# Sums over features by token in a Hyena and DeltaNet layer: which operand of the product is stationary

## Chip, core and metric

The kernel runs on one core of a Trainium2 chip (trn2). The metric is the device time of one execution in microseconds; three runs give 3350.19, 3352.44 and 3355.91 us, and their median, 3352.44 us, is the time before.

## What is computed

One trunk layer is applied to 128 context tokens and 256 latent tokens, 384 in all, of 2048 features each: a half-step SwiGLU, a token mixer (Hyena and gated DeltaNet side by side) and a second half-step SwiGLU. Each sub-layer stands between two RMS norms, and in the DeltaNet q and k are normalised per head:

```python
def rms_norm(x, g):
    y = xf * lax.rsqrt(jnp.mean(xf * xf, axis=-1, keepdims=True) + RMS_EPS)
    return (y * g.astype(jnp.float32)).astype(x.dtype)

def l2_norm(x):
    return x * lax.rsqrt(jnp.sum(x * x, axis=-1, keepdims=True) + RMS_EPS)

def trunk_layer(...):
    h = adaln(x, norm_pre[0], mod[:, :, 0], mod[:, :, 1])
    x = x + 0.5 * mod[:, :, 2] * rms_norm(swiglu(h, ...), norm_post[0])
    h = adaln(x, norm_pre[1], mod[:, :, 3], mod[:, :, 4])
    ...    # y: Hyena (with a norm of its own) and DeltaNet, times w_out
    x = x + mod[:, :, 5] * rms_norm(y, norm_post[1])
    h = adaln(x, norm_pre[2], mod[:, :, 6], mod[:, :, 7])
    x = x + 0.5 * mod[:, :, 8] * rms_norm(swiglu(h, ...), norm_post[2])
```

All inputs are float32. The change concerns the sums over features that these norms need.

## The kernel before

Activations lie with features on the partitions: a tile is 128 features by 384 tokens (T), and 16 tiles (KT) make the 2048 features. Weights come from DRAM in units of 512 rows by 256 columns (`unit`, line 122 and below), are split into two float32r parts, `hi` (ScalarE, line 122) and `lo` (VectorE or GpSimd, line 123), and each product of 128 x 128 weights with a tile is three TensorE instructions, lines 146 to 148, of 384 columns each.

The stages in order of time are: the start up to about 190 us (loading and transposing x, the first norm, the modulation's first quarter-blocks, lines 285 to 298, and the filter spectra of the Hyena between them), the first FFN, a bridge, the Hyena (to about 1630 us), the DeltaNet scans of four pairs of heads, the output projection `w_out`, a second bridge, the second FFN and the output.

A sum over features runs across partitions, so TensorE does it. Three places need one:

- `rms` (line 353) for the norm of x at the start (16 tiles) and the Hyena's output norm (8 tiles, line 1166). ScalarE squares a tile (line 361), and TensorE multiplies it by a stationary block of ones of 32 columns (line 363), each tile to one of four quarters of the partitions of one PSUM bank. Then the sums are copied to SBUF (line 365), three products with a column of constants bring them to one value per token (line 368), GpSimd raises these to the power -1/2 (line 371), and `spread` (line 445) copies them to all partitions.
- `fold` and `fold_end`: beside the last down-projection of the first FFN (fold 1), beside `w_out` (fold 2) and beside the last down-projection of the second FFN (fold 3). For each tile of the result y, folds 1 and 2 sum y^2, x y' and y'^2 (lines 418, 427, 429), one kind to each quarter of the partitions; tiles 0 to 11 are first added in pairs on GpSimd (line 437), and the last four tiles go singly. That makes 30 sums. Fold 3 has 16 sums of y^2 alone. The product is in `add_sum`, line 412. `fold_end` copies the sums out (line 454), transposes them to tokens (line 465; in fold 3 line 460) and computes the factors on VectorE and GpSimd (lines 461 to 473). `bridge` spreads them, updates x and makes the operands of the next sub-layer.
- `gdn_pair`: squared norms of q and k of two heads, four tiles (line 825), copied (827), transposed (829) and used from line 833 on.

In the down-projection the sums of one step of 256 columns are handed out behind the products of the next step, so those of the last four tiles stand behind the last product. The program is written in order and a scheduler of the framework, which has its own model of durations, sets the order on each engine. Every engine takes its instructions in that order. The modulation's weight blocks (512 KB) go through a ring of four buffers (`aw`, line 285) on SP's DMA queue.

Of the kernel before, what the change touches and what calls it, by code (L numbers as in the profile page):

```python
# [19 lines left out]
P = 128  # L20
# [24 lines left out]
def constants():  # L45
    """Tables that depend on the shapes alone."""
# [23 lines left out]
    # per level the couples within a block of 2s whose halves differ  # L70
# [10 lines left out]
    # Transforms at the odd frequencies pi (f + 1/2) / n, where the products of a signal's and a filter's lags below n  # L81
    # don't wrap. The latent ones take the even and the odd tokens apart: they give f and, with the other sign, n - 1 - f.
# [22 lines left out]
class Builder:  # L105
# [19 lines left out]
    def unit(self, src, cols=256):  # L125
        """Rows (k p) x columns of a weight, as two float32r parts whose sum is the weight."""
# [23 lines left out]
    def proj(self, mats, xh, xl, order=(0, 1, 2, 3)):  # L150
        """For each (weight, first column): two tiles [128 features, T] of weight^T x; with a third entry, the
        number of columns, one tile of so many features."""
        mats = [(m + (256,))[:3] for m in mats]
        res = [[self.acc() for _ in range(max(1, m[2] // P))] for m in mats]
        for a, kg in enumerate(order):
            us = [self.unit(w[kg * 512:kg * 512 + 512, c0:c0 + n], n) for w, c0, n in mats]
            for k in range(4):
                kk = kg * 4 + k
                for pts, u, m in zip(res, us, mats):
                    for n, pt in enumerate(pts):  # L160
                        wd = min(P, m[2])
# [5 lines left out]
    def setup(self):  # L167
# [5 lines left out]
        small = cst.tile([P, 4], F32, name="small")  # L173
        nc.vector.memset(small[:, 0:1], 2.0 ** -16)
        nc.vector.memset(small[:, 1:2], 2.0 ** -15)
        nc.vector.memset(small[:, 2:4], -0.5)
        self.c_d, self.c_dh = small[:, 0:1], small[:, 1:2]
# [18 lines left out]
        # groups of at most 128 rows for a transpose each, the first of the conditioning alone  # L196
# [27 lines left out]
        # silu of the conditioning, as the stationary operand of the modulation (columns: context, latent)  # L224
# [129 lines left out]
    def rms(self, pool, get, n, const, ring):  # L354
        """The mean square over features plus eps, per token, [128, 3], and its -1/2nd power for every partition, [128, T]
        in PSUM; get(i): the i-th of n tiles."""
        nc = self.nc
        ps = self.aux("sums")
        for i in range(n):
            sq = ring()  # L360
            nc.scalar.activation(out=sq, in_=get(i), func=AF.Square)
            q = 32 * (i % 4)
            nc.tensor.matmul(ps[q:q + 32, :T], self.ones[:, :32], sq, start=i < 4, stop=i >= n - 4)
        sb = ring()
        nc.vector.tensor_copy(out=sb, in_=ps[:, :T])
        pt = self.aux("tok")
        for t in range(3):
            nc.tensor.matmul(pt[:, t:t + 1], sb[:, t * P:t * P + P], const, start=True, stop=True)
        r = pool.tile([P, 2, 3], F32, tag="r6", name="r6", bufs=1)
        nc.vector.tensor_scalar(out=r[:, 0], in0=pt[:, :3], scalar1=EPS, scalar2=None, op0=ALU.add)  # L370
# [3 lines left out]
    def coef(self, pool, i):  # L374
        """Scale of the i-th pre-norm, [128, group, KT]."""
# [30 lines left out]
        # the modulation's accumulator is free  # L406
# [4 lines left out]
    def add_sum(self, q, first, last, sq):  # L411
        self.nc.tensor.matmul(self.f["ps"][32 * q:32 * q + 32, :T], self.ones[:, :32], sq, start=first, stop=last)  # L412

    def fold(self, k, y):
        """What tile k of y adds to the sums."""
# [3 lines left out]
        if f["last"]:  # L419
            for v, (a, b) in enumerate(SEG):  # L420
                nc.vector.tensor_scalar(out=y[:, a:b], in0=y[:, a:b], scalar1=f["pg"][:, v, k:k + 1], scalar2=None, op0=ALU.mult)
            return [(k % 4, k < 4, k >= KT - 4, sq)]
# [8 lines left out]
        if k < KT - 4:  # L431
            # TensorE takes the sums of two tiles
# [6 lines left out]
        return [(q, k < 2, k == KT - 1, a) for q, a in enumerate(new)]  # L439

    def spread(self, r):
        """[128 tokens, 3] -> the same for every partition, [128, T] in PSUM."""
# [5 lines left out]
    def fold_end(self):  # L448
        """Per token: factor of the post-norm and, but for the last, of the pre-norm after it."""
        nc, f = self.nc, self.f  # L450
        tt, ts, st = nc.vector.tensor_tensor, nc.vector.tensor_scalar, nc.vector.scalar_tensor_tensor
        n = P if f["last"] else 96
        sb = f["ring"]()
        nc.vector.tensor_copy(out=sb[:n], in_=f["ps"][:n, :T])
        pt = self.aux("tok")
        r = f["pool"].tile([P, 3, 3], F32, tag="r3", name="r3", bufs=1)
        r1, r2, s = r[:, 0], r[:, 1], r[:, 2]
        if f["last"]:
            for t in range(3):
                nc.tensor.matmul(pt[:, t:t + 1], sb[:, t * P:t * P + P], self.c_d, start=True, stop=True)  # L460
            ts(out=s, in0=pt[:, :3], scalar1=EPS, scalar2=None, op0=ALU.add)
            nc.gpsimd.tensor_tensor(out=r1, in0=s, in1=self.mhalf[:, :3], op=ALU.pow)
            return r1, None
# [4 lines left out]
        nc.gpsimd.tensor_tensor(out=r1, in0=s, in1=self.mhalf[:, :3], op=ALU.pow)  # L468
        tt(out=s, in0=m[:, :, 2], in1=r1, op=ALU.mult)
# [6 lines left out]
    def bridge(self, pool, x, y, i):  # L476
        """x += r1 y', and the operands of the next sub-layer, the i-th, a tile of features at a time."""
# [109 lines left out]
    def sine(self, out, x, bias):  # L587
        """out = sin(x + bias), the argument brought to [-pi, pi] first."""
# [16 lines left out]
    def filters(self, pool, loads):  # L605
        """Filter spectra of both sequence lengths, without their normalisation, into DRAM; its inverse stays. Yields between its
        parts."""
# [14 lines left out]
        def last_layer(o, half):  # L622
            """The last layer's columns of a filter and half of the channels, both directions, twice."""
# [16 lines left out]
        # the second layer's output twice, on either half of the partitions: [h; h] and its float32r parts [hi; hi], [lo; 0]  # L640
# [28 lines left out]
            # sum and difference of both directions: context, even and odd latent tokens  # L669
# [56 lines left out]
    def conv3(self, u, pt, w):  # L726
        """u = centred width-3 convolution along the tokens of pt, within each group; w(j): [128, 1]."""
# [8 lines left out]
    def gates(self, pl, pt):  # L736
        """Decay and beta of every (direction, chunk, head), per token, and what the chunks need of them."""
# [20 lines left out]
        # softplus(x) = max(x, 0) + 2 atanh(e / (2 + e)) with e = exp(-|x|)  # L758
# [33 lines left out]
    def gdn_pair(self, pl, p, hh, hl, out):  # L792
        """q, k and v of a pair of heads and what its scan needs of them, into out; yields after q and after k."""
# [5 lines left out]
        # one slot of 24 KB holds, for two pairs in turn, q and k by feature and k and v by token  # L799
# [7 lines left out]
        for i in range(3):  # L807
# [20 lines left out]
            for t in range(3):  # L828
                nc.tensor.transpose(pn[:, t * P:t * P + P], sq[:, t * P:t * P + P], self.ident)
# [499 lines left out]
```

## Time and profile before

| what | value |
|---|---|
| median of three runs | 3352.44 us |
| profiled execution, first to last instruction | 3349.9 us |
| TensorE busy (matmul) | 3268.2 us, 98% |
| VectorE busy | 2150.9 us, 64% |
| ScalarE busy | 1109.6 us, 33% |
| GpSimd busy | 228.5 us, 7% |
| TensorE's clock, mean of what was granted | 0.989 |

PE stands for TensorE's matmuls and PEld for its loading of the stationary operand, which overlaps them; DVE is VectorE, ACT is ScalarE, POOL is GpSimd and SP issues DMAs. Products are pipelined, so their durations overlap, and a busy share of 98% does not say how densely they are issued: for that the starts of neighbours are compared. A float32 product of this kernel appears as two instructions in the trace; a float32r product and a transpose appear as one.

### The profile page before, as it was taken

The numbers are of one execution on the slowest core, as the hardware profiler recorded it, in microseconds if no ns is written. First come the engines' busy times: TensorE is split into PE (matmuls) and PEld (weight loads), VectorE is DVE, ScalarE is ACT, GpSimd is POOL, SyncE is SP. The second block draws the span as 40 slices with busy tenths as digits, with TensorE's granted clock in tenths as the row PEclk, the third lists the DMA queues.
The fourth block names the chain that finished last, engine by engine and source line by source line (L and its number), as shares of the span: only waits on it lengthen the run. The fifth ranks groups of instructions, "written<-read, shape, count | busy, mean of one in ns | idle before, by whom it ended". The sixth has DMA issues, their size and how long they took to land.

```text
span 3349.9 us, 47713 instructions
## 1 busy us (share of the span) xinstructions
PE 3268.2 (98%) x19174; PEld 3098.8 (93%) x19174; DVE 2150.9 (64%) x3042; ACT 1109.6 (33%) x1602; POOL 228.5 (7%) x249
## 2 busy tenths in 40 slices
PE   5899999999999999999999999989999999999998
PEld 2499999999999997999999999979999999999997
DVE  4579978879786957777656665479544433444434
ACT  4432222222222225433333333353222222222223
POOL 1100000000000003100122321120000000000000
PEclk8999999999999999999999999999999999999999
DMA  9867767667665742543322234338444333444442
GB/s 308 289 200 251 251 193 227 220 203 247 225 220 175 253 143 82 180 124 113 120 76 70 76 95 145 112 109 268 149 129 128 126 126 126 126 127 126 129 129 83
DMA packets 423798, 542.71 MB, mean 162 GB/s; under 512 B 20292, under 2 KB 373882, under 8 KB 422936
## 3 DMA queue, kind: packets, MB, share of 16 engines
q1 hardware_dynamic: 413072, 522.27, 48.8%
q10 hardware_dynamic: 8232, 11.40, 1.0%
q0 software_dynamic: 2272, 5.98, 0.6%
q8 instruction: 151, 2.47, 0.3%
q14 instruction: 71, 0.58, 0.1%
HBM read 524.38 MB, written 15.20 MB: 161 GB/s over the span
## 4 chain that ended last, share of the span: by engine, by line
PE 92%; DVE 4%; DMA 2%; issue 1%; ACT 1%; POOL 0%; ACTq 0%; DVEq 0%; SPq 0%; POOLq 0%
PE mm L146 27%; PE mm L148 27%; PE mm L147 27%; DMA aw<-in_ada_w_dram 2%; PE sums L412 1%; PE pb L1058 1%; PE pb L1053 1%; PE ada L291 1%; DVE acc L327 1%; DVE lo L123 1%; PE aux L1100 1%; PE aux L1124 1%; PE pa L334 1%; DMA slot<-in_hy_decay_dram 1%; PE aux L716 0%
## 5 line engine op out<-in xcount | busy, mean ns | idle before, releaser
L123 DVE TENSOR_TENSOR lo<-raw,hi 128x1024 fp32r<-128x1024 f32 (+1 forms) x676 | 825.8, 1223 | 679.7 <-ACT hi L122 664.5
L146 PE MATMUL mm<-hh,hi 128*128 128x384 f32 x3728 | 1247.8, 338 | 7.6 <-ACT hh L122 6.3
L147 PE MATMUL mm<-hl,hi 128*128 128x384 f32 x3728 | 1253.1, 336 | 0.7 <-POOL hl L123 0.3
L122 ACT CAST hi<-raw 128x1024 fp32r<-128x1024 f32 (+1 forms) x676 | 707.3, 1047 | 1617.6 <-PE mm L147 1460.1
L148 PE MATMUL mm<-hh,lo 128*128 128x384 f32 x3728 | 1238.8, 337 | 2.4 <-DVE lo L123 2.4
L146 PEld LDWEIGHTS mm<-hh,hi 128*128 128x128 f32 x3728 | 700.2, 188 | 18.5 <-ACT hh L122 8.2
L148 PEld LDWEIGHTS mm<-hh,lo 128*128 128x128 f32 x3728 | 699.2, 188 | 13.1 <-issue 6.7
L147 PEld LDWEIGHTS mm<-hl,hi 128*128 128x128 f32 x3728 | 701.1, 188 | 8.8 <-issue 4.9
L327 DVE SCALAR_TENSOR_TENSOR acc<-aw,cs,acc 128x1024 f32<-128x1024 f32 x420 | 519.4, 1277 | 33.7 <-DMA aw<-in_ada_w_dram 33.0
L148 PE MATMUL mm<-gh,lo 128*128 128x384 f32 x1408 | 472.7, 336 | 1.5 <-DVE lo L123 1.5
L146 PE MATMUL mm<-gh,hi 128*128 128x384 f32 x1408 | 474.1, 337 | 0.0
L147 PE MATMUL mm<-gl,hi 128*128 128x384 f32 x1408 | 472.1, 335 | 0.0
L538 DVE TENSOR_TENSOR yacc<-mm,yacc 128x384 f32<-128x384 f32 x320 | 171.4, 554 | 166.5 <-PE mm L148 166.5
L146 PEld LDWEIGHTS mm<-gh,hi 128*128 128x128 f32 x1408 | 264.3, 188 | 13.7 <-issue 7.7
L148 PEld LDWEIGHTS mm<-gh,lo 128*128 128x128 f32 x1408 | 264.2, 188 | 7.8 <-issue 5.0
L147 PEld LDWEIGHTS mm<-gl,hi 128*128 128x128 f32 x1408 | 264.3, 188 | 2.5 <-issue 2.5
L437 POOL TENSOR_TENSOR sqs<-sqs 128x384 f32<-128x384 f32 x36 | 44.3, 1241 | 1174.3 <-DMA raw<-in_ffn_wd_dram 1080.1
L148 PE MATMUL mm<-yh,lo 128*128 128x384 f32 x256 | 85.8, 339 | 0.0
L147 PE MATMUL mm<-yl,hi 128*128 128x384 f32 x256 | 85.8, 336 | 0.0
L513 ACT ACTIVATE sg<-mm 128x384 f32<-128x384 f32 x88 | 43.3, 492 | 127.4 <-PE mm L148 127.3
L146 PE MATMUL mm<-yh,hi 128*128 128x384 f32 x256 | 85.0, 337 | 0.0
L291 PE MATMUL ada<-aw,cs 128*32 128x256 f32 x512 | 51.6, 445 | 25.9 <-DMA aw<-in_ada_w_dram 19.4
(327 smaller groups left out, 2263.7 us busy)
## 6 DMA issues: line engine op xcount, KB each, us to landing
aw<-in_ada_w_dram SPq DMA_DIRECT2D x288, 512.0 KB, 4.5
raw<-in_ffn_wg_dram SPq DMA_DIRECT2D x176, 512.0 KB, 3.6
raw<-in_ffn_wu_dram SPq DMA_DIRECT2D x176, 512.0 KB, 3.9
raw<-in_ffn_wd_dram SPq DMA_DIRECT2D x176, 512.0 KB, 3.4
raw<-in_w_in_dram SPq DMA_DIRECT2D x112, 512.0 KB, 3.5
raw<-in_w_out_dram SPq DMA_DIRECT2D x32, 512.0 KB, 3.3
spec<-fev ACTq DMA_DIRECT2D x24, 256.0 KB, 5.9
sp<-spec SPq DMA_DIRECT2D x8, 768.0 KB, 6.1
```

What stands on the lines that cost most here:

```text
L122: self.nc.scalar.copy(out=hi, in_=src)
L123: return (eng or self.nc.vector).tensor_tensor(out=lo, in0=src, in1=hi, op=ALU.subtract)
L146: t.matmul(out, hi[:, k, c], xh, start=first, stop=False)
L147: t.matmul(out, hi[:, k, c], xl, start=False, stop=False)
L148: t.matmul(out, lo[:, k, c], xh, start=False, stop=last)
L291: nc.tensor.matmul(pa[q:q + 32, :256], self.cs[:, kt, :], aw[:, m, h * 256:h * 256 + 256], start=kt == 0, stop=kt == KT - 1)
L327: nc.vector.scalar_tensor_tensor(out=d, in0=aw, scalar=self.cs[:, kt, v:v + 1], in1=d, op0=ALU.mult, op1=ALU.add)
L334: nc.tensor.matmul(pa[32 * q:32 * q + 32, :], self.pick[:, v], acc[:, v, q * 512:q * 512 + 512], start=v == 0, stop=v == 1)
L412: self.nc.tensor.matmul(self.f["ps"][32 * q:32 * q + 32, :T], self.ones[:, :32], sq, start=first, stop=last)
L437: nc.gpsimd.tensor_tensor(out=a, in0=a, in1=b, op=ALU.add)
L513: nc.scalar.activation(out=sg, in_=pg[n], func=AF.Silu)
L538: nc.vector.tensor_tensor(out=y, in0=pts[n], in1=y, op=ALU.add)
```

## The change

`token_sum` takes the place of the product with the block of ones. The tile of squares is the stationary operand, 128 tokens of it at a time, and one column of ones moves, so three products give the sums of a tile with the tokens on the partitions, one column per 128 tokens. The kinds of sums lie in neighbouring columns of a bank instead of quarters of the partitions, and all tiles accumulate into the same columns. The copies to SBUF and the transposes or products with constants behind them go, and so do the constants; the factor 1/n is applied in the VectorE instruction that adds EPS. Comments and docstrings go too, so line numbers differ.

```diff
-    def rms(self, pool, get, n, const, ring):
+    def token_sum(self, ps, c, sq, first, last):
+        for t in range(3):
+            self.nc.tensor.matmul(ps[:, c + t:c + t + 1], sq[:, t * P:t * P + P], self.ones[:, :1],
+                                  start=first and t == 0, stop=last and t == 2)
+
+    def rms(self, pool, get, n, ring):
         for i in range(n):
             sq = ring()
             nc.scalar.activation(out=sq, in_=get(i), func=AF.Square)
-            q = 32 * (i % 4)
-            nc.tensor.matmul(ps[q:q + 32, :T], self.ones[:, :32], sq, start=i < 4, stop=i >= n - 4)
-        sb = ring()
-        nc.vector.tensor_copy(out=sb, in_=ps[:, :T])
-        pt = self.aux("tok")
-        for t in range(3):
-            nc.tensor.matmul(pt[:, t:t + 1], sb[:, t * P:t * P + P], const, start=True, stop=True)
+            self.token_sum(ps, 0, sq, i == 0, i == n - 1)
...
     def add_sum(self, q, first, last, sq):
-        self.nc.tensor.matmul(self.f["ps"][32 * q:32 * q + 32, :T], self.ones[:, :32], sq, start=first, stop=last)
+        self.token_sum(self.f["ps"], 3 * q, sq, first, last)
...
     def fold_end(self):
-        sb = f["ring"]()
-        nc.vector.tensor_copy(out=sb[:n], in_=f["ps"][:n, :T])
-        pt = self.aux("tok")
...
-        for t in range(3):
-            nc.tensor.transpose(pt[:, t * 96:t * 96 + 96], sb[:n, t * P:t * P + P], self.ident[:n, :n])
-        m = pt[:, :288].rearrange("p (t q c) -> p t q c", t=3, q=3)[:, :, :, 0]
+        m = f["ps"][:, :9].rearrange("p (q t) -> p t q", q=3)
...
     def gdn_pair(self, pl, p, hh, hl, out):
             for m in range(4):
...
-                mm(pn[32 * m:32 * m + 32, :T], self.ones[:, :32], sq, start=True, stop=True)
-            sq = pl.tile([P, T], F32, tag="th", name="gsq", bufs=2)
-            nc.scalar.copy(out=sq, in_=pn[:, :T])
-            for t in range(3):
-                nc.tensor.transpose(pn[:, t * P:t * P + P], sq[:, t * P:t * P + P], self.ident)
+                self.token_sum(pn, 3 * m, sq, m == 0, m == 3)
```

The scheduler orders the engines anew. On TensorE at the first sums of fold 1 (`mm` is a bank of the down-projection, `sums` that of the fold, `sqs` the squares), before:

```order
L146 MATMUL mm<-gh,hi 128x384
L147 MATMUL mm<-gl,hi 128x384
L412 MATMUL sums<-sqs,base 32x384
L148 MATMUL mm<-gh,lo 128x384
L146 MATMUL mm<-gh,hi 128x384
L147 MATMUL mm<-gl,hi 128x384
L148 MATMUL mm<-gh,lo 128x384
L412 MATMUL sums<-sqs,base 32x384
```

and now, where line 353 is the product in `token_sum`:

```order
L146 MATMUL mm<-gh,hi 128x384
L147 MATMUL mm<-gl,hi 128x384
L353 MATMUL sums<-base,sqs 128x1 x9
L148 MATMUL mm<-gh,lo 128x384
L146 MATMUL mm<-gh,hi 128x384
```

The three sums of a pair of tiles, which stood apart, follow each other as nine products. At the end of fold 1, on TensorE behind the last products of the FFN, before:

```order
L148 MATMUL mm<-gh,lo 128x384
L412 MATMUL sums<-sqs,base 32x384 x12
L465 MATMUL tok<-base,sqs 128x96 x3
L445 MATMUL rb<-base,r_10909 128x128 x6
L146 MATMUL mm<-hh,hi 32x384
```

and now:

```order
L148 MATMUL mm<-gh,lo 128x384
L353 MATMUL sums<-base,sqs 128x1 x36
L441 MATMUL rb<-base,r_10990 128x128 x6
L146 MATMUL mm<-hh,hi 32x384
```

The transposes are gone, and the twelve sums are 36 products at the same place. At the start, on TensorE (`ada` is the modulation, `aw` its weight blocks, `rb` the spread factor), before:

```order
L363 MATMUL sums<-early,base 32x384 x3
L291 MATMUL ada<-aw,cs 32x256 x4
L363 MATMUL sums<-early,base 32x384 x2
L368 MATMUL tok<-small,early 128x1 x3
L291 MATMUL ada<-aw,cs 32x256 x4
L445 MATMUL rb<-base,r_288 128x128 x3
```

and now:

```order
L353 MATMUL sums<-base,early 128x1 x6
L286 MATMUL ada<-aw,cs 32x256 x3
L353 MATMUL sums<-base,early 128x1 x3
L293 MATMUL ada<-base,asb 128x128 x2
L286 MATMUL ada<-aw,cs 32x256 x14
L441 MATMUL rb<-base,r_311 128x128 x3
```

The spread (line 445, now 441) stands behind 14 products of the modulation and its first two transposes instead of four products.

## Rows read from the trace of the kernel before

**Rows 1.** Page, part 4: share of the chain that ended last, by engine.

```profile
PE 92%; DVE 4%; DMA 2%; issue 1%; ACT 1%; POOL 0%; ACTq 0%; DVEq 0%; SPq 0%; POOLq 0%
```

**Rows 2.** Stretches: us, busy us (instructions) by engine, TensorE's clock, DMA share, GB/s.

```profile
500.00:1270.00 770.00, 767.62 (x4423) 753.02 (x4421) 609.31 (x647) 220.83 (x253) 4.15 (x4) 1.00 0.66 211
...
1700.00:1800.00 100.00, 97.93 (x658) 92.05 (x657) 66.79 (x173) 36.96 (x77) 28.35 (x34) 1.00 0.23 69
...
1900.00:2010.00 110.00, 106.91 (x732) 100.68 (x731) 71.31 (x179) 39.31 (x84) 34.18 (x40) 1.00 0.27 82
```

**Rows 3.** Timeline of PE, fold 1: start us, us, engine, line, op, out<-in, count.

```profile
1276.26 0.34 PE L146 MATMUL mm<-gh,hi 128*128 128x384 f32 x1
1276.53 0.83 PE L412 MATMUL sums<-sqs,base 128*32 128x384 f32 x2
...
1277.57 0.34 PE L148 MATMUL mm<-gh,lo 128*128 128x384 f32 x1
```

**Rows 4.** Timeline of PE, fold 2.

```profile
2104.86 0.34 PE L147 MATMUL mm<-yl,hi 128*128 128x384 f32 x1
2105.13 0.84 PE L412 MATMUL sums<-sqs,base 128*32 128x384 f32 x4
...
2106.18 0.34 PE L146 MATMUL mm<-yh,hi 128*128 128x384 f32 x1
```

**Rows 5.** Timeline of PE, second use of `rms`.

```profile
1594.68 0.34 PE L148 MATMUL mm<-hh,lo 128*128 128x384 f32 x1
1594.85 0.72 PE L368 MATMUL tok<-small,sq 128*128 128x1 f32 x6
...
1595.70 0.34 PE L147 MATMUL mm<-hl,hi 128*128 128x384 f32 x1
```

**Rows 6.** Timeline of PE, norms of the first pair of heads.

```profile
1643.50 0.34 PE L146 MATMUL mm<-hh,hi 128*128 128x384 f32 x1
1643.68 0.49 PE L829 MATMUL pn<-base,gsq 128*128 128x128 f32 x3
...
1644.18 0.34 PE L148 MATMUL mm<-hh,lo 128*128 128x384 f32 x1
```

**Rows 7.** Timeline of all engines, end of fold 1.

```profile
1310.94 2.98 PE L412 MATMUL sums<-sqs,base 128*32 128x384 f32 x24
...
1315.07 0.16 DVE L467 TENSOR_SCALAR r<-tok 128x3 f32<-128x3 f32 x1 [0.56 <-PE tok L465]
```

**Rows 8.** Timeline of all engines, end of fold 3.

```profile
3331.99 0.83 PE L412 MATMUL sums<-sqs,base 128*32 128x384 f32 x2
...
3336.05 0.80 PE L460 MATMUL tok<-small,sqs 128*128 128x1 f32 x6 [0.27 <-DVE sqs L454]
3336.89 0.16 DVE L461 TENSOR_SCALAR r<-tok 128x3 f32<-128x3 f32 x1 [0.98 <-PE tok L460]
```

**Rows 9.** Timeline of all engines, end of fold 2.

```profile
2193.92 2.63 PE L412 MATMUL sums<-sqs,base 128*32 128x384 f32 x12 [1.38 <-ACT sqs L418]
...
2197.70 0.16 DVE L467 TENSOR_SCALAR r<-tok 128x3 f32<-128x3 f32 x1 [0.56 <-PE tok L465]
...
2200.58 1.65 PE L445 MATMUL rb<-base,r 128*128 128x128 f32 x6 [0.78 <-POOL r L473]
```

**Rows 10.** Timeline of all engines, the first norm.

```profile
50.63 0.85 PE L363 MATMUL sums<-early,base 128*32 128x384 f32 x3
...
60.07 0.64 PE L291 MATMUL ada<-aw,cs 128*32 128x256 f32 x8
...
61.36 0.94 PE L445 MATMUL rb<-base,r 128*128 128x128 f32 x6 [0.66 <-POOL r L371]
...
62.34 0.56 DVE L1210 COPY rb<-rb 128x384 f32<-128x384 f32 x1 [2.00 <-PE rb L445]
```

**Rows 11.** Page, part 6: DMA issues, KB each, median us from issue to landing.

```profile
aw<-in_ada_w_dram SPq DMA_DIRECT2D x288, 512.0 KB, 4.5
```

**Rows 12.** Stretches, after the end of fold 1.

```profile
1318.00:1320.00 2.00, 1.61 (x6) 1.31 (x6) 1.46 (x4) 0.00 (x0) 0.00 (x0) 0.50 0.00 0
```

More of the change, by code (lines that the diff above doesn't have):

```diff
@@ L172, in setup @@
         self.ident, self.ones = base[:, 0:P], base[:, P:2 * P]
[L173 to L177, printed above, removed]
         self.pick = cst.tile([P, 2, 32], F32, name="pick")
@@ L361, in rms @@
             nc.scalar.activation(out=sq, in_=get(i), func=AF.Square)
-            q = 32 * (i % 4)
-            nc.tensor.matmul(ps[q:q + 32, :T], self.ones[:, :32], sq, start=i < 4, stop=i >= n - 4)
-        sb = ring()
-        nc.vector.tensor_copy(out=sb, in_=ps[:, :T])
-        pt = self.aux("tok")
-        for t in range(3):
-            nc.tensor.matmul(pt[:, t:t + 1], sb[:, t * P:t * P + P], const, start=True, stop=True)
+            self.token_sum(ps, 0, sq, i == 0, i == n - 1)
         r = pool.tile([P, 2, 3], F32, tag="r6", name="r6", bufs=1)
-        nc.vector.tensor_scalar(out=r[:, 0], in0=pt[:, :3], scalar1=EPS, scalar2=None, op0=ALU.add)
+        nc.vector.tensor_scalar(out=r[:, 0], in0=ps[:, :3], scalar1=1.0 / (n * P), scalar2=EPS, op0=ALU.mult, op1=ALU.add)
         nc.gpsimd.tensor_tensor(out=r[:, 1], in0=r[:, 0], in1=self.mhalf[:, :3], op=ALU.pow)
@@ L421, in fold @@
                 nc.vector.tensor_scalar(out=y[:, a:b], in0=y[:, a:b], scalar1=f["pg"][:, v, k:k + 1], scalar2=None, op0=ALU.mult)
-            return [(k % 4, k < 4, k >= KT - 4, sq)]
+            return [(0, k == 0, k == KT - 1, sq)]
         xy = f["ring"]()
@@ L438, in fold @@
             new = f["even"]
-        return [(q, k < 2, k == KT - 1, a) for q, a in enumerate(new)]
+        return [(q, k == 1 and q == 0, k == KT - 1 and q == 2, a) for q, a in enumerate(new)]
     def spread(self, r):
@@ L451, in fold_end @@
         tt, ts, st = nc.vector.tensor_tensor, nc.vector.tensor_scalar, nc.vector.scalar_tensor_tensor
-        n = P if f["last"] else 96
-        sb = f["ring"]()
-        nc.vector.tensor_copy(out=sb[:n], in_=f["ps"][:n, :T])
-        pt = self.aux("tok")
         r = f["pool"].tile([P, 3, 3], F32, tag="r3", name="r3", bufs=1)
         r1, r2, s = r[:, 0], r[:, 1], r[:, 2]
-        if f["last"]:
-            for t in range(3):
[L460 to L463, printed above, removed]
-        for t in range(3):
-            nc.tensor.transpose(pt[:, t * 96:t * 96 + 96], sb[:n, t * P:t * P + P], self.ident[:n, :n])
-        m = pt[:, :288].rearrange("p (t q c) -> p t q c", t=3, q=3)[:, :, :, 0]
+        m = f["ps"][:, :9].rearrange("p (q t) -> p t q", q=3)
         ts(out=s, in0=m[:, :, 0], scalar1=1.0 / D, scalar2=EPS, op0=ALU.mult, op1=ALU.add)
         nc.gpsimd.tensor_tensor(out=r1, in0=s, in1=self.mhalf[:, :3], op=ALU.pow)
+        if f["last"]:
+            return r1, None
         tt(out=s, in0=m[:, :, 2], in1=r1, op=ALU.mult)
@@ L824, in gdn_pair @@
                 nc.scalar.activation(out=sq, in_=qkv[:, m // 2, m % 2], func=AF.Square)
-                mm(pn[32 * m:32 * m + 32, :T], self.ones[:, :32], sq, start=True, stop=True)
-            sq = pl.tile([P, T], F32, tag="th", name="gsq", bufs=2)
-            nc.scalar.copy(out=sq, in_=pn[:, :T])
-            for t in range(3):
-                nc.tensor.transpose(pn[:, t * P:t * P + P], sq[:, t * P:t * P + P], self.ident)
+                self.token_sum(pn, 3 * m, sq, m == 0, m == 3)
             nk = pl.tile([P, 2, 3, 2], F32, tag="nk", name="nk", bufs=2)
@@ L832, in gdn_pair @@
             fl = lambda a: a.rearrange("p i t h -> p (i t h)")
-            ts(out=nk, in0=pn[:, :T].rearrange("p (t i n c) -> p i t n c", t=3, i=2, n=2)[:, :, :, :, 0], scalar1=EPS, scalar2=None, op0=ALU.add)
+            ts(out=nk, in0=pn[:, :12].rearrange("p (i h t) -> p i t h", i=2, h=2), scalar1=EPS, scalar2=None, op0=ALU.add)
             nc.gpsimd.tensor_tensor(out=fl(rk), in0=fl(nk), in1=self.mhalf[:, :12], op=ALU.pow)
@@ L1165, in hyena @@
             part(i, q)
-        _, rb = self.rms(pl, lambda k: ymix[:, k], 8, self.c_dh, lambda: pl.tile([P, T], F32, tag="sq", name="sq", bufs=5))
+        _, rb = self.rms(pl, lambda k: ymix[:, k], 8, lambda: pl.tile([P, T], F32, tag="sq", name="sq", bufs=5))
         hn = self.vec["hnorm"]
@@ L1207, in run @@
                 next(load, None)
-                self.xx, r = self.rms(self.cst, lambda k: x[:, k], KT, self.c_d, itertools.cycle([early(T) for _ in range(3)]).__next__)
+                self.xx, r = self.rms(self.cst, lambda k: x[:, k], KT, itertools.cycle([early(T) for _ in range(3)]).__next__)
                 rb = sp.tile([P, T], F32, name="rb")
```

## The prediction

> **What bounds the kernel now.** I read the chain of waits first: 92% of the span is work of TensorE and hardly anything else stands on it [rows 1]. The table of stretches says the same by stage: in the body of the first FFN 4423 TensorE instructions fill 770 us, 0.174 us each, and in two stretches of the DeltaNet scans TensorE is busy for 97.9 of 100 and 106.9 of 110 us [rows 2]. So over most of the program an edit is worth what it changes in TensorE's own issue time, start to start, and the duration column (0.33 us for a product that is followed by the next after 0.174 us) is no price, because products overlap. Next I read the timeline of TensorE around the old operation, to price it inside the stream: start of the last product before it, start of the second product after it, less two steps of 0.174 us. Three places have another limit, and there I followed the waits: the start, the two bridges between sub-layers, and the last microseconds.
>
> **Prices.** One sum of a tile as it is (two passes of a 32-column stationary ones block, 384 columns moving) costs 1277.57 - 1276.26 - 0.35 = 0.96 us in the stream [rows 3]. Two sums in different quarters of the partitions cost 1.32 - 0.35 = 0.97 us together, thus as much as one [rows 4]. The new form stands in the trace already: in line 368 a tile is the stationary operand, 128 tokens at a time, and one column moves. Its three products are six instructions and cost 1595.70 - 1594.68 - 0.35 = 0.67 us [rows 5], about 0.112 us an instruction; further ones in a row add 0.67 us for each sum, since nothing in this form shares the array. So a lone sum gains 0.29 us, and a pair that ran at once loses 2 x 0.67 - 0.97 = 0.37 us. The program makes 76 sums in the folds (30, 30 and 16), 24 in the norms and 16 for q and k.
> The Trainium skill (TensorE: Matmul & The Clock Gate, "Part 3: Packing small matmuls") says that small products whose outputs lie in different quarters of the partitions run at the same time, which speaks against giving the quarters up. Rows 4 agree, 0.97 us for two. Were it so for every tile's three sums, fold 1 below would have cost 6 x 0.97 = 5.8 us before and the change would come out 11.5 us worse than my sum; rows 3 show a sum of fold 1 alone.
>
> **The change part by part.**
> *Norms of q and k (four pairs of heads).* The first pair has four lone sums and three transposes; the others two lone sums, two at once and the transposes. The three transposes of line 829 cost 1644.18 - 1643.50 - 0.35 = 0.33 us [rows 6]. Before: 4 x 0.96 + 0.33 = 4.2 us, and three times 0.97 + 1.92 + 0.33 = 3.2 us, 13.8 us in all; after: 16 x 0.67 = 10.7 us. The stage is dense [rows 2]: **-3.1 us**. The order of the inverses around it changes too; that is a rival.
> *Fold 1, inside the last down-projection.* Before, the order has 18 lone sums there: 18 x 0.96 = 17.3 us. After, they come as nine products each, 18 x 0.67 = 12.1 us: **-5.2 us**, if GpSimd's additions for the pair are ready for three sums at once. TensorE and the additions both move with the projection by one weight block, so I expect no wait.
> *End of fold 1.* The last twelve sums stand after the last product, before and after. Before, they used three quarters at once, and from their start to the first step on the result (line 467) it took 1315.07 - 1310.94 = 4.13 us, copy and transposes included [rows 7]. After, 36 products are 72 instructions: line 460's six take 0.84 us until line 461 starts [rows 8], so 0.84 + 66 x 0.112 = 8.2 us; copy and transposes are gone in it. **+4.1 us**; nothing else is there for TensorE to do.
> *Second norm of the mixer (line 1166).* One lone sum gains 0.3 us, line 368's six instructions go (0.7 us), seven sums in a row are 4.7 us, about what they occupy now with their waits (bounds -1 and +1): **-0.7 us**. The factor's way gets shorter, but projections cover it.
> *Fold 2.* 24 sums in 17 groups, 17 x 0.96 = 16.4 us, become 24 x 0.67 = 16.1 us. The last six took 2197.70 - 2193.92 = 3.8 us to line 467 [rows 9], and take 6 x 0.67 + 0.25 = 4.3 us. **0 us.**
> *Fold 3.* Five pairs and two lone sums, 6.8 us, become 12 x 0.67 = 8.0 us; at the end the copy and line 460 go. From the first of the last four sums to line 461 it is now 4.9 us (3331.99 to 3336.89), of which four sums, one group of transposes (0.5 us) and the step's start remain: 2.7 + 0.5 + 0.25 = 3.5 us, 1.4 less against 1.2 more. **-0.2 us** [rows 8].
> *The start.* The first norm's 16 sums are 16 x 0.67 = 10.7 us of TensorE, and more blocks of the modulation and two transposes now stand ahead of the spread. Now the sums begin at 50.63 and the spread starts at 61.36; a block of the modulation, four products in eight instructions, takes 0.64 us [rows 10]. By the new order 22 products of the modulation stand between the sums, so the last sum ends near 50.6 + 10.7 + 5.5 x 0.64 = 64.8 us, and with the factor's steps and 14 further products the spread comes near 67, 5 us later. On VectorE the copy of the factor (line 1210) at 62.34 stands ahead of the filters' products (line 681) in both orders [rows 10], so these start 5 us later as well. Blocks of the modulation are issued some 1.5 us later at that place, and that stream ends the stage. I charge **+1.5 us**, nearest to its own delay; bounds: -2 (VectorE or DMA would have waited anyway) and +6 (the filters hold it back in full).
> Sum: -3.1 - 5.2 + 4.1 - 0.7 + 0 - 0.2 + 1.5 = -3.6 us on the profiled 3349.9 us. That execution lies 2.5 us under the median of the runs, 3352.44, so I carry the difference over: 3348.9, said as **3349 us**. Scratch copies on VectorE and ScalarE that go (nine of about 0.5 us) are counted only where the end waited for them.
>
> **Rivals.** *Faster than by the sum.* The scans' inverses have stretches with no projection between, where the chain through the other engines sets the pace; in the two stretches shown TensorE is idle for 2.1 + 3.1 = 5.2 us [rows 2]. If the norms, which come earlier, take 4 us of that away and the start costs nothing, it is -3.6 - 4 - 1.5 = -9 us: 3343 us. For it: the scale of k is what the first step of an inverse waits for, and copy and transposes go from its way; against: by the new order the three chunks of pair 0 go in lockstep, which may add waits as easily.
> *Slower: the ring of the modulation's blocks.* SP loads a block only when TensorE has freed the one four before; from issue to landing it takes 4.5 us [rows 11]. TensorE takes its instructions in order, so whenever it is held by a filter product whose PSUM the late VectorE has not freed, the four loaded blocks run out and a journey of 4.5 us is paid. The filters start 5 us later; if the new order pays the journey three times, the start costs +13.5 instead of +1.5 us: -3.6 + 12 = +8.4, 3361 us. It decides from two journeys lost on. Against it: the order now lets 14 products of the modulation go ahead of the spread.
> *The clock in the long burst.* After the burst of fold 1 TensorE waited, and the granted clock was at its lower level, 0.50, from 1318 to 1320 [rows 12]. Six products of the spread take 0.94 us at the higher level and 1.65 us at the lower [rows 10, 9], so a one-column instruction would go from 0.112 to some 0.20 us, an estimate. If the clock falls half way through the 72, it is 36 x 0.09 = +3.2 us: 3352 us, no change. The Trainium skill (TensorE: Matmul & The Clock Gate, "What's actually happening") has the clock follow how busy the array is; no run here shows whether one-column products keep it up.
> *The change does not make sums cheaper.* Where they ran two or three at once it doesn't, and that is in the sum. If in fold 1 TensorE waits 0.9 us at each of the six places for GpSimd's third addition, its 5.2 us are gone: 3354 us, no change.
>
> **How the numbers follow.** 0.2% is 6.7 us, about what a measurement of this kernel can tell from no change (the three runs before lie 5.7 us apart). Forecast 3349: 0.32; the clock 0.14 and the wait in fold 1 0.08, both within 0.2%; faster 0.27; slower by the ring 0.19. So faster 0.27, same 0.54, slower 0.19. The range runs from 3339 (the faster case with both of its gains a bit larger) to 3362 us (the slower case's 3361 just inside); the likeliest case's own range is 3345 to 3354 us.
>
> **What would show it.** In the profile after: sums of line 352 in steps of 0.67 us; fold 1's body shorter by 5 us and its burst 8 us long at granted clock 1.00; line 452 straight behind the last sum, with no copy; the spread near 67 us and the modulation's last block no more than 2 us later than now; the stage of the scans 3 us shorter. A burst over 9 us at a lower clock, waits for DMA in the first 170 us, or more idle time in the inverses would make the forecast wrong.

## The result, and the profile after the change

The change makes the kernel slower: 3368.61 us (median of four runs, 3365.87 to 3371.95) against 3351.95 us (3350.19 to 3355.91). The ratio is 1.0052, 95% interval 1.0038 to 1.0066: 16.7 us more, where 3349 was forecast and 3362 was the upper end of the range. The profiled execution of after took 3368.23 us, with a span of 3366.2 us against 3349.9 us.

The page of after shows nothing special at first: TensorE still has 98% of the span, and the chain is still nine tenths TensorE, as in [rows 1]. The one line that speaks is that of the granted clock, with an 8 among the nines at the 16th and at the 27th slice, where folds 1 and 2 end:

```profile
span 3366.2 us, 48567 instructions
...
PE 3294.0 (98%) x19602; PEld 3181.8 (95%) x19602; DVE 2146.9 (64%) x3034; ACT 1105.5 (33%) x1598; POOL 222.1 (7%) x249
...
PEclk7999999999999998999999999989999999999999
```

To see where the time went I took the 16,176 products of the projections, which both programs execute in the same number, and compared the start of the n-th in either trace. The table gives how much later (+) or earlier (-) the program came out of each stage than before, worked out in the same way for two kernels: after, and the wide experiment that is told below.

| Stage (us in the trace of before) | forecast | after | wide |
|---|---|---|---|
| start and the beginning of FFN 1 (0 to 681) | +1.5 | +5.5 | -3.0 |
| FFN 1, where no sum stands (to 1268) | 0 | +1.6 | +1.7 |
| fold 1, body (to the last product, 1310.7) | -5.2 | -5.7 | -5.7 |
| end of fold 1, bridge, mixer's first part (to 1500) | +4.1 | +6.8 | +3.4 |
| second norm, first pair's q and k (to 1641) | -0.7 and a part of -3.1 | +1.3 | -1.9 |
| scans (to 2070) | the rest of -3.1 | -1.5 | -1.6 |
| fold 2, body (to 2172) | 0 | +5.6 | -0.7 |
| end of fold 2 and bridge (to 2321) | together with the body | +2.8 | +0.8 |
| FFN 2, fold 3, end (the last by the spans) | -0.2 | -0.1 | +0.1 |

The body of fold 1 and the scans came out as forecast. The loss stands in the start, at the end of fold 1, in the second norm and in fold 2. Each column compares one execution with one of before, so a figure of a few us can be chance: the parts of the wide run add up to -7 us where its medians, below, say -1.5 (the profiled execution is its fastest), and the +1.6 us in FFN 1, where no sum stands, is explained by nothing here.

**The start.** First two stretches of before, 50 to 60 and 60 to 70 us (us, busy us and instructions by engine in the order PE, PEld, DVE, ACT, POOL, then the clock, the DMA share and GB/s), and below them the same two of after with the one that follows:

```profile
50.00:60.00 10.00, 9.32 (x66) 4.23 (x66) 2.24 (x4) 7.47 (x16) 0.00 (x0) 1.00 0.97 343
60.00:70.00 10.00, 9.29 (x78) 4.20 (x77) 6.18 (x15) 5.32 (x12) 1.40 (x2) 1.00 0.79 263
```

```profile
50.00:60.00 10.00, 9.96 (x68) 8.71 (x68) 1.75 (x3) 5.53 (x11) 0.00 (x0) 0.70 0.85 301
60.00:70.00 10.00, 10.00 (x55) 7.56 (x52) 0.00 (x0) 2.62 (x6) 0.00 (x0) 0.50 0.37 106
70.00:80.00 10.00, 10.00 (x57) 5.90 (x55) 0.60 (x5) 0.37 (x1) 0.88 (x1) 0.50 0.48 143
```

TensorE is busy all the time and does less: 55 instructions in ten microseconds instead of 78, at clock 0.50, the lower of its two levels (1.2 GHz). The DMA share falls with it; TensorE, which frees the modulation's blocks, gets through fewer of them. TensorE's timeline of after in the same place (start us, us, line, operation, out<-in, count):

```profile
50.70 1.47 PE L353 MATMUL sums<-base,early 128*128 128x1 f32 x12
52.09 0.64 PE L286 MATMUL ada<-aw,cs 128*32 128x256 f32 x8
52.66 6.60 PE L353 MATMUL sums<-base,early 128*128 128x1 f32 x36
59.20 1.08 PE L286 MATMUL ada<-aw,cs 128*32 128x256 f32 x8
...
74.38 1.44 PE L353 MATMUL sums<-base,early 128*128 128x1 f32 x6
...
79.84 1.65 PE L441 MATMUL rb<-base,r 128*128 128x128 f32 x6
```

Twelve one-column instructions take 1.47 us, as priced; of the next 36 the first 14 start 0.112 us apart and the others 0.214 us, and from there on everything on TensorE is slow, the modulation's products too (eight of them 1.08 instead of 0.64 us). The sums end near 75.7 us instead of the 64.8 of the forecast, and the spread starts at 79.84 instead of 67 (61.36 before, [rows 10]).

**The end of fold 1.** Timeline and stretches of after:

```profile
1312.29 11.07 PE L353 MATMUL sums<-base,sqs 128*128 128x1 f32 x72
...
1323.39 0.16 DVE L451 TENSOR_SCALAR r<-sums 128x3 f32<-128x3 f32 x1 [8.23 <-PE sums L353]
```

```profile
1312.30:1317.30 5.00, 5.00 (x46) 5.00 (x45) 2.53 (x4) 2.16 (x4) 0.00 (x0) 0.97 0.18 43
1317.30:1323.40 6.10, 6.06 (x29) 5.97 (x28) 0.01 (x1) 0.00 (x0) 0.00 (x0) 0.50 0.16 55
```

The 72 instructions run at 0.112 us for the first 5 us, then the clock falls, and they take 11.1 us instead of 8.2 us to the step that reads them, which answers to line 467 in [rows 7] (4.13 us after the first sum there).

**The second norm.** Timeline of after:

```profile
1589.86 5.66 PE L353 MATMUL sums<-base,sq 128*128 128x1 f32 x42
1595.38 0.67 PE L146 MATMUL mm<-hh,hi 128*128 128x384 f32 x1
1595.85 0.52 PE L147 MATMUL mm<-hl,hi 128*128 128x384 f32 x1
1596.16 0.52 PE L148 MATMUL mm<-hh,lo 128*128 128x384 f32 x1
```

The last nine of the 42 start 0.214 us apart, and the projection's products behind them 0.32, until the clock rises at 1600.3 us.

**Fold 2.** Timeline of after, and the stretch that follows the 18 instructions:

```profile
2088.52 0.72 PE L353 MATMUL sums<-base,sqs 128*128 128x1 f32 x6
...
2090.23 2.38 PE L353 MATMUL sums<-base,sqs 128*128 128x1 f32 x18
2092.47 0.67 PE L146 MATMUL mm<-yh,hi 128*128 128x384 f32 x1
2092.94 0.52 PE L147 MATMUL mm<-yl,hi 128*128 128x384 f32 x1
2093.26 0.52 PE L148 MATMUL mm<-yh,lo 128*128 128x384 f32 x1
...
2094.86 1.27 PE L353 MATMUL sums<-base,sqs 128*128 128x1 f32 x6
```

```profile
2092.00:2104.00 12.00, 12.00 (x43) 12.00 (x44) 1.42 (x2) 1.04 (x1) 2.00 (x2) 0.50 0.38 124
```

Here the dearest part is not the sums. The clock falls at the end of the 18 and stays at 0.50 until 2105.5 us; in that time the projection's own products start 0.32 us apart instead of 0.174. Where 18 such instructions stood between longer runs of products, as later in fold 2 and in the body of fold 1, the clock held and they cost 2.01 us, three times the 0.67 of the forecast:

```profile
1277.12 2.06 PE L353 MATMUL sums<-base,sqs 128*128 128x1 f32 x18
1279.05 0.42 PE L148 MATMUL mm<-gh,lo 128*128 128x384 f32 x1
```

At the end of fold 2 there are two runs of 36. The first, at 2190.3 us, keeps its steps of 0.112 us, and the clock falls for the products right behind it; the second, after a wait of 1.72 us, slows to 0.213 us half way.

### The profile page after: what moved, and what is told of

Read it like the earlier page. It is cut to its first block, busy times and chain, and to the rows that moved or that the text cites. A ratio compares the mean times of both kernels' runs of the same rounds, so it can differ in the third digit from the quotient of the medians.

```text
span 3366.2 us, 48567 instructions
## 1 busy us (share of the span) xinstructions
PE 3294.0 (98%) x19602; PEld 3181.8 (95%) x19602; DVE 2146.9 (64%) x3034; ACT 1105.5 (33%) x1598; POOL 222.1 (7%) x249
## 4 chain that ended last, share of the span: by engine, by line
PE 91%; DVE 5%; DMA 2%; issue 1%; ACT 1%; POOL 0%; ACTq 0%; DVEq 0%; SPq 0%; POOLq 0%
PE mm L146 27%; PE mm L148 26%; PE mm L147 26%; PE sums L353 2%; DMA aw<-in_ada_w_dram 1%; DVE acc L322 1%; PE pb L1040 1%; PE ada L286 1%; DVE lo L123 1%; PE pb L1035 1%; PE aux L1106 1%; PE aux L1082 1%; PE pa L329 1%; DMA slot<-in_hy_decay_dram 1%; PE aux L702 0%
```

## The experiments

The theory after reading the traces: the price of 0.112 us for a one-column instruction holds only at the higher clock; runs of them let the clock fall, and the lower clock is then paid by them and by whatever follows. The first rival was the one of the prediction: the late spread and filters make the start wait for blocks of the modulation. The second: the program is in another order, and other places lose time. Differences to before are always to runs of before made beside them on the same chip, and these medians, 3348.5 to 3349.3 us, lie about 3 us under the 3351.95 of the result.

**The norms of q and k alone.** The kernel before, with only this:

```diff
-    mm(pn[32 * m:32 * m + 32, :T], self.ones[:, :32], sq, start=True, stop=True)
-sq = pl.tile([P, T], F32, tag="th", name="gsq", bufs=2)
-nc.scalar.copy(out=sq, in_=pn[:, :T])
-for t in range(3):
-    nc.tensor.transpose(pn[:, t * P:t * P + P], sq[:, t * P:t * P + P], self.ident)
+    self.token_sum(pn, 3 * m, sq, m == 0, m == 3)
```

> The kernel before with the new form in the norms of q and k alone. The clock theory (runs of one-column products let TensorE's clock fall, and that costs the time; where the clock stays up the new form has its price of 0.67 us a sum): 16 sums at 0.67 us and no transposes, clock 1.00 through the scans, so -3.1 us as in the prediction: 3348 to 3350 us. The rival that the new order of the scans costs as much as the norms give: 3352 to 3355 us.

Measured 3347.65 us against 3349.33, ratio 0.9993 (0.9985 to 1.0002): -1.7 us, with an interval from -5.0 to +0.7. That holds the -3.1 us and leaves no room for a loss of 3 us; by itself it can't be told from no change. By the products of the projections, the stretch from 1500 to 2070 us is 2.6 us shorter than in before. The same profile shows how far a start can differ without a change: this kernel has the first norm of before, and is 3.7 us earlier at 681 us.

**The first norm in the old form.** The kernel after, with `rms` of before for the first norm:

```diff
-self.xx, r = self.rms(self.cst, lambda k: x[:, k], KT, ...)
+self.xx, r = self.rms_old(self.cst, lambda k: x[:, k], KT, self.c_d, ...)
```

> The kernel after with the first norm in the old form (sums in quarters, copy, three products with a constant), all else new. In the two traces the first FFN runs 5.5 us later after the change. If the first norm alone does that, the time falls from 3368.6 to 3362 us (-5.5 to -7), the granted clock of 50 to 70 us is 1.00 again and the spread comes near 62 us. If the start is late for another reason (the folds' memory or order), it stays at 3366 to 3369 us.

Measured 3360.33 us against 3349.33, ratio 1.0028 (1.0017 to 1.0038): 11.0 us over before instead of 16.7, so the first norm is worth 5.7 us by the medians, and 4.9 by the place of the two programs at 681 us. The clock of 50 to 70 us is 1.00, the spread starts at 61.0 us, and the start comes out 0.6 us later than in before. The 5.7 us are loose: executions of this kernel lie 15.6 us apart (3349.91 to 3365.53), the profiled one is the slowest, and by the interval the first norm is worth 4 to 11 us. The fastest has a mean granted clock of 0.989, as before has, and the slowest 0.981; so it seems that executions of one program differ in how often the clock falls in the folds, though only the slowest left a trace. The run shows where about a third of the loss sits; it doesn't tell the clock from the late filters.

**The same instructions with more columns.** The kernel after, with 128 moving columns of ones in `rms` and 56 in the folds:

```diff
-def token_sum(self, ps, c, sq, first, last):
+def token_sum(self, ps, c, sq, first, last, w=1):
     for t in range(3):
-        self.nc.tensor.matmul(ps[:, c + t:c + t + 1], sq[:, t * P:t * P + P], self.ones[:, :1], ...)
+        o = (c + t) * w
+        self.nc.tensor.matmul(ps[:, o:o + w], sq[:, t * P:t * P + P], self.ones[:, :w], ...)
```

> The kernel after with the same products in the same number, but with more columns of ones moving: 128 in the norms by rms, 56 in the folds (the extra columns of the result are copies that nobody reads). The clock theory: the columns lie under the weight loads (128 columns are a third of a 384-column product, 0.058 us against a step of 0.112), the clock stays near 1.00 in the start's sums and in the bursts of the folds, the steps of 0.214 us go back to 0.112, the start's sums end near 65 us instead of 75, and the time falls from 3368.6 to 3352 to 3358 us. The rival (the number of instructions and the late filters behind them set the loss, not the clock): 3366 to 3372 us, with steps as before.

Measured 3347.85 us against 3349.33, ratio 0.9994 (0.9985 to 1.0003): -1.5 us (-5.0 to +1.0). The whole loss is gone, and a little more than expected. Its stretches, then its timeline at the start:

```profile
50.00:60.00 10.00, 10.00 (x96) 8.40 (x95) 0.19 (x1) 5.94 (x12) 0.00 (x0) 1.00 0.95 325
60.00:70.00 10.00, 9.70 (x90) 5.66 (x92) 3.88 (x12) 3.93 (x10) 1.40 (x2) 1.00 0.77 247
```

```profile
51.22 4.29 PE L352 MATMUL sums<-base,early 128*128 128x128 f32 x36
...
62.98 0.94 PE L352 MATMUL sums<-base,early 128*128 128x128 f32 x6
...
65.14 0.94 PE L440 MATMUL rb<-base,r 128*128 128x128 f32 x6
```

And at the end of fold 1 and in fold 2:

```profile
1303.80 8.14 PE L352 MATMUL sums<-base,sqs 128*128 128x56 f32 x72
```

```profile
2074.99 2.11 PE L352 MATMUL sums<-base,sqs 128*128 128x56 f32 x18
2076.91 0.42 PE L146 MATMUL mm<-yh,hi 128*128 128x384 f32 x1
2077.18 0.33 PE L147 MATMUL mm<-yl,hi 128*128 128x384 f32 x1
```

The 36 instructions that took 6.60 us take 4.29, the 72 that took 11.07 take 8.14, and the products behind the 18 start 0.174 us apart again. The extra columns cost nothing: the steps stay at 0.112 us, so up to 128 columns what moves doesn't set the step. The expectation's 0.058 us for 128 columns is too small, since it comes from a float32r product; by the 0.322 us that a float32 pass of 384 columns takes (below) they are 0.107 us, an estimate, just under the step, and no run here tried more. The rival of instruction counts and late filters falls: the number of instructions is the same, the spread is still later than in before (65.1 against 61.4 us), and the start loses nothing; the DMA share from 60 to 70 us is 0.77 again. One reservation: at the start the scheduler also puts the later blocks of the modulation elsewhere between the sums. The 72 at the end of fold 1 and the 42 of the second norm stand as in after, so there the columns alone make the difference. One clock loss stays in this kernel: in the burst at the end of fold 2, which comes after a wait of 1.7 us, the last eight steps are 0.21 us.

**Fold 2 in the old form.** The kernel after, with the folds' old code for the mixer's output projection alone:

```diff
+if self.f["old"]:
+    self.nc.tensor.matmul(self.f["ps"][32 * q:32 * q + 32, :T], self.ones[:, :32], sq, start=first, stop=last)
+else:
     self.token_sum(self.f["ps"], 3 * q, sq, first, last)
```

> The kernel after with the second fold (the mixer's output projection) in the old form, all else new. Between the two traces 7 to 8 us are lost from 2080 to 2270 us. The clock theory: these come from fold 2's own sums and from products beside them at the lower clock (0.32 instead of 0.174 us a step from 2092 to 2100 us), so 3368.6 falls to 3360 to 3362 us, clock 1.00 from 2090 to 2110 us. The rival (the mixer's end is late for what happens before it, and the fold has only its linear price of about 0): 3367 to 3369 us.

Measured 3358.79 us against 3349.33, ratio 1.0026 (1.0017 to 1.0036): 9.5 us over before instead of 16.7, so fold 2 is worth 7.2 us by the medians, inside the 7 to 8 us that were to be explained. By the products its body costs 0.0 us (5.6 in after), and the stretch of 2090 to 2110 us is at clock 1.00 instead of 0.66, first in after, then in this run:

```profile
2090.00:2110.00 20.00, 20.00 (x92) 20.00 (x91) 4.64 (x6) 3.01 (x4) 2.80 (x2) 0.66 0.25 79
```

```profile
2090.00:2110.00 20.00, 20.00 (x102) 16.19 (x101) 9.11 (x14) 6.57 (x12) 4.28 (x3) 1.00 0.32 106
```

Its first norm has the form of after, and its start is late again, by 6.4 us. The rival that the mixer's end is late for other reasons falls.

**More columns in the norms by `rms` alone.** The wide edit with one column left in the folds.

> The kernel after with 128 moving columns of ones in the two uses of rms (the first norm and the mixer's second norm), one column in the folds and in the norms of q and k. The clock theory: the start's sums end near 65 us at clock 1.00 and 8 us of the 16.7 go (the old form in the first norm gave 8), the second norm gives another 1 to 1.5, and the folds lose as much as before: 3358 to 3361 us. The rival that the wide form wins by something else than the clock in the start (the run with wide operands everywhere won 20 us): well below 3357 us or above 3364.

Measured 3359.70 us against 3348.49, ratio 1.0032 (1.0020 to 1.0044): 11.2 us over before. That is inside the range in microseconds, but by luck: the expectation's 8 us for the first norm is the difference of two times that weren't measured beside each other (by the runs of before beside them it is 5.7), and against before 5.5 of the 16.7 us went where 9 or more were expected. The trace bears the parts out:

```profile
67.00 0.93 PE L440 MATMUL rb<-base,r 128*128 128x128 f32 x6
```

The spread starts at 67.0 us, just where the forecast had it, the clock of 50 to 70 us is 1.00, and the start comes out 1.0 us earlier than in before; the stretch with the second norm goes from +1.3 to -1.9 us. The folds lose about what they lose in after (16.0 us against 15.1 by the products, from the end of fold 1 to its bridge and in fold 2). So a spread that is 5.6 us late costs the start nothing that shows beside the 3.7 us by which starts differ anyway. In after it is 18 us late and the modulation's products are slow as well; which of the two brings the 5.5 us isn't separated, but both come from the clock.

**Another stationary operand.** Could sums be cheaper than either form? Built on the kernel before, all sums with 128 stationary columns and 384 moving; the transposes behind the sums of folds 1 and 2 and of q and k become products with three or four columns of the identity:

```diff
-self.nc.tensor.matmul(self.f["ps"][32 * q:32 * q + 32, :T], self.ones[:, :32], sq, ...)
+self.nc.tensor.matmul(self.f["ps"][:, :T], self.ones if self.f["last"] else self.sel[:, 3 - q:3 - q + P], sq, ...)
```

> Another form of all sums, built on the kernel before: the squares move as before, 384 columns, but the stationary operand has all 128 columns (one column of ones among zeros, or ones throughout for the norms by rms), so nothing changes to quarters of the array and the columns are many. By the rows of before a sum of 0.96 us has only 0.35 us of its own two passes of 384 columns; the rest is the entry and exit at the change of form. If that is what it is, a sum costs 0.35 us: fold 1 -11 and +1.5 at its end, second norm -2, fold 2 -8, fold 3 -2.6, q and k 16 x 0.35 + 4 x 0.67 = 8.3 against 13.8: -27 us, near 3322 us from 3349.3. If every change between these sums and the products of the projections costs the same entry and exit, lone sums stay at 0.96 us: 3343 to 3350 us. The clock stays at 1.00 in both.

> As the run with the full-width stationary operand, but the norms of q and k in the one-column form, which needs no copy on ScalarE: 10.7 us of TensorE instead of 8.3 there, so 2.4 us more by the sum, 3324 to 3325 us. If the copy stands on the inverses' way, it is the same or faster than that run.

Both expectations fell: 3358.33 us (ratio 1.0029, 1.0018 to 1.0040) and, with the one-column form for q and k, 3356.26 us (1.0020, 1.0011 to 1.0028). The timeline of the first, in the body of fold 1 and at its end:

```profile
1272.89 0.81 PE L414 MATMUL sums<-sqs,sel 128*128 128x384 f32 x2
1273.24 0.63 PE L148 MATMUL mm<-gh,lo 128*128 128x384 f32 x1
1273.71 0.34 PE L146 MATMUL mm<-gh,hi 128*128 128x384 f32 x1
...
1307.69 7.90 PE L414 MATMUL sums<-sqs,sel 128*128 128x384 f32 x24
```

The error was to take 0.174 us for a pass of 384 columns in float32. The starts of the two passes lie 0.322 us apart, so a lone sum costs 0.65 us: of the old 0.96 us, two thirds are the passes themselves and only 0.32 us the change of form. The Trainium skill (FP8 and Floating Point Precision, "TensorE Precision Notes") has true float32 as four passes through the array; the trace nearly agrees, with 0.64 us for the two instructions against 0.174 for one float32r pass below, 3.7 times as long. Twenty-four such instructions in a row take 7.9 us, about as long as the 72 one-column instructions at the higher clock, so at its end fold 1 loses again (+5.2 us by the products). From 1641 to 2070 us the second kernel gains 1.3 us on before and the first loses 3.6, although by the expectation it asks 2.4 us less of TensorE. The copy on ScalarE doesn't show as the cause: until 1776 us (in the trace of before) the first has gained 2.4 us, and by 1807 it has lost 6.2. In between no projection stands, and TensorE waits 2.9 us in all, against 1.9 in before; the longest wait is for VectorE,

```profile
1784.68 0.75 PE L1060 MATMUL pb<-yg,zc 128*128 128x128 f32 x4 [1.78 <-DVE zc L1057]
```

and from 1786 to 1793 us the clock is 0.50, where before has 1.00. Whether the copy, earlier on, makes VectorE late there stays open.

**The folds in float32r.** The second of these kernels, with the folds' squares and products written as float32r, so that their sums are one pass:

```diff
-sqs = ada.tile([P, 2, D], F32, tag="acc", name="sqs", bufs=1)
+sqs = ada.tile([P, 2, D], F32R, tag="acc", name="sqs", bufs=1)
-self.nc.tensor.matmul(self.f["ps"][:, :T], self.ones if ... else self.sel[...], sq, ...)
+self.nc.tensor.matmul(self.f["ps"][:, :T], self.selr[:, 3 - q:3 - q + P], sq, ...)
```

> As the run before it, with the fold's sums in float32r: the squares and products are rounded when they are written, and a sum is one pass of 384 columns, 0.174 us, instead of two. 76 sums x 0.174 = 13 us less where TensorE is the limit, 3311 us; if GpSimd's additions or the writing engines set the end of the folds, 3316 to 3324 us.

Measured 3326.37 us against 3348.49, ratio 0.9932 (0.9920 to 0.9945), 22 us less than before. A sum in the stream costs a step like any product:

```profile
1273.59 0.34 PE L422 MATMUL sums<-sqs,selr 128*128 128x384 f32 x1
1273.76 0.33 PE L148 MATMUL mm<-gh,lo 128*128 128x384 f32 x1
```

It missed the 3311 us: at the ends of folds 1 and 2 TensorE now waits for the writing engines (steps of 0.3 to 2 us between the last sums), as the second half of the expectation had it, though 2 us beyond its range. Fold 1 gains 14.6 us in its body and fold 2 9.5.

**The best of both.** The same, with the squares stationary and 128 columns of ones moving in the two uses of `rms`.

> The folds' sums as float32r with the full-width stationary operand (3326.4 us in the run with that alone), the norms of q and k in the one-column form, and the two uses of rms with the squares stationary and 128 columns of ones moving. The full-width float32 sums of those two norms took two steps of 0.322 us each, as long as six steps of 0.112; what goes are the copy, six instructions (0.67 us) and their wait, twice. If the first norm's end is on the start's path, 2 to 5 us less: 3321 to 3324 us, clock 1.00 in the start's sums. If the start has its end from DMA and the filters anyway: 3325 to 3327 us.

Measured 3321.12 us against 3348.71, ratio 0.9918 (0.9904 to 0.9931), 27.6 us less than before, at clock 0.990 and a span of 3317.7 us. The spread, first in the run above, then here:

```profile
68.33 0.93 PE L456 MATMUL rb<-base,r 128*128 128x128 f32 x6
```

```profile
65.97 0.94 PE L450 MATMUL rb<-base,r 128*128 128x128 f32 x6
```

It starts at 66.0 us instead of 68.3, and at 681 us this kernel is 1.9 us ahead of the kernel before, the run above 4.2 us behind; the two other kernels with the full-width first norm are 3.0 and 3.5 us behind. That fits a first norm on the start's path, but by the spans only 2.4 of the 5.2 us are left at the end, and starts differ by 3.7 us without a change: how much of the gain is the norm's stays open. This version beats both kernels; it rounds the folds' squares and products to float32r, which neither of them does.

## Why the prediction was wrong

- **The failed step is the price of 0.112 us an instruction, used at every place.** It came from six instructions among products [rows 5], at clock 1.00, and was carried to runs of 36, 42 and 72. The clock rival had the mechanism and the size of a slow step (0.20 us as an estimate, 0.214 measured), but I gave it one place, +3.2 us, and counted it as no change. It applied at four, and the forecast's chance for it should have stood on the slower side.
- **The start** was charged +1.5 us, with bounds -2 and +6; it came out at +5.5 in the profile and 5.7 us by the run with the old form, inside the bounds by luck: it got there by another way than both the charge and the slower rival. With more columns its landmarks were those of the forecast (last sums at 63.6 and 65.5 us, spread at 65.1 and 67.0), and the cost was nothing that shows.
- **Fold 2** was said to cost 0. At the higher clock that is right: -0.7 and +0.8 us in the wide run. In after it cost 8.4 us, and most of it in products of the projection behind the sums, a term that the sum didn't have at all: I had priced what a slow sum costs, and not what a lowered clock costs the work that follows.
- **The end of fold 1**, +4.1: 8.2 us for the burst at the higher clock was right (8.14 us with more columns); 11.1 us were paid. The clock rival's +3.2 us for this place is the 2.9 us measured.
- **The second norm**, -0.7: the stretch came out at +1.3 us. 42 instructions stand in a row there, and the last nine of them and the products behind ran at the lower clock; with more columns the stretch is 3.2 us shorter.
- **Body of fold 1**, -5.2: -5.7, in each kernel with the new form there. The three products of a sum cost 0.67 us, and GpSimd was in time, so the rival that TensorE waits for it falls. **q and k**, -3.1: -2.6 by the trace of the run with that alone. Its sums cost 0.67 us one by one and 1.17 to 1.34 us two at a time.
- **The ring of the modulation's blocks**, the slower rival, fell as it was put: with a spread 5.6 us late at the higher clock the start lost nothing. In after the DMA share does fall to 0.37 between 60 and 70 us, while TensorE works at the lower clock; whether a spread 18 us late costs journeys besides isn't shown. **The faster rival** (the inverses' waits) showed nothing beyond the sum.

Two slips of the text change nothing: the lines 352 and 452 to look for are 353 and 451 of the kernel after, and 3352.44 less 3.6 is 3348.8.

Taken at the higher clock the working was sound: the wide kernel does all that the change meant, and lies 1.5 us under before (-5.0 to +1.0) where the sum said 3.6. What stays open is why the clock held through 18 one-column instructions at some places and fell at others. The order of instructions alone doesn't decide it: the same 72 at the end of fold 1 ran at the higher clock for 4.7 us in after, and for 2.9 to 3.7 us in the three runs that have them in the same form; the first 36 at the end of fold 2 ran whole at 0.112 us in after and slowed half way in two of these.

## What to carry to other kernels

A price measured on a few instructions among dense products belongs to their clock. Before carrying it to a long run of very narrow products, look at the granted clock of the place, and price a fall twice: in the run itself and in the dense work behind it. Where the step of a narrow product doesn't depend on how many columns move (here up to 128), more of them are free and can keep the clock up; and where the rounding can be borne, it pays to ask first whether the sum can be an ordinary full-width product in a one-pass type.

## What the runs showed of the hardware

- A busy TensorE is not enough for its clock. From 60 to 70 us of after it is busy for 10.00 of 10 us and granted 0.50. The Trainium skill (TensorE: Matmul & The Clock Gate, "What's actually happening") has the clock set by how busy the array has been; the busy column of the profile can't stand for that, because one-column products fill it while the clock falls.
- With one, 56 or 128 moving float32 columns a product with 128 stationary columns starts every 0.112 us at the higher clock. At the lower one it was 0.214 us with one column.
- A float32 pass of 384 columns takes 0.322 us from start to start, a float32r pass 0.174. A lone float32 sum in a quarter of the array costs 0.96 us, with the whole array 0.65, as three one-column products 0.67, and as a float32r pass 0.174.
